# Issuing a gate row's strip products of two weight quarters in a row

## The chip, the cores and the metric

One core of one Trainium2 chip runs the whole program. The metric is the device time of one execution in microseconds (us). The kernel before took 604.39 us, the median of three runs that lay between 603.84 and 604.91 us.

## The reference, cut to what matters

The program is one step of a hybrid trunk layer: a modulated RMS norm, one input projection for two parallel head groups (a gated position-mixing group and a latent attention group), a joint output projection, and a gated residual. Nine tiles of 128 tokens pass through it, eight of latent tokens and one of context tokens. The part that the change touches is the gate:

```python
mod = jax.nn.silu(cond) @ w_ada + b_ada
shift, scale, gate = jnp.split(mod[:, None, :], 3, axis=-1)
...
return x + gate * y
```

`cond` is one vector of 1024 numbers for the latent tokens and another one for the context tokens, `w_ada` is 1024 x 3072. The gate is the last third of the result: two rows of 1024 numbers, one for each condition. Nothing needs it before the output projection at the end of the program.

## The kernel before

The work runs in stages. In the first, the tokens are normed, transposed and modulated, and shift and scale come out of the first two thirds of `w_ada`. In the channel stage twelve chunks of 128 input-projection columns (`w2r` is a raw chunk of 512 KB, `w` its two halves of high and low bits) are multiplied with the modulated tokens, two chunks at a time, as seven sums of products (`p`: p1 to p7) and two plain products for the last three token tiles (`tp`). After that come the wide products (`zacc`), attention, and the output projection.

Every product in the channel stage is a matmul with a 128 x 128 stationary tile and 384 moving columns; a product of fp32 quality is made of three passes. Their results lie in six PSUM banks (pool `psa`). Two further banks (pool `pst`) serve short jobs.

The gate is worked out inside the channel stage, in four quarters of 256 columns, one at a time, by `gate_steps(j)` from line 996 on. One quarter goes as follows.

- `fetch`, lines 1004 to 1008: SyncE's queue loads the quarter of the weights (`adag`, 1 MB) and its bias (`grow`, 2 KB). The pool `vg` has one buffer for `adag`.
- `strips`, lines 1010 to 1014: eight matmuls, one for each 128 rows of the quarter. The stationary tile `csp` is only 32 columns wide (two conditions, the rest zeros), so four of them stand beside each other in the array, and their results go to four strips of 32 partitions of one `pst` bank (`gps`). The trace shows each of these fp32 matmuls as two.
- `high` on ScalarE (line 1018, tile `hig`) and `low` on VectorE (the helper in line 112, tile `log`) split the strips into two parts.
- `total`, line 1026: two matmuls against a selecting matrix add the four strips up to two rows, in the other half of the same bank.
- `out`, lines 1029 and 1030: VectorE adds the bias, and a DMA writes the two rows to the DRAM tensor `gdram`, from where the output projection reads them back at 515 us and later.

The order on each engine is fixed when the program is written out. A planner (class `Plan`, from line 42) takes steps with an engine, an assumed cost, dependences and a priority, and runs through assumed time; whenever an engine is free it writes out the first ready step in order of priority. The real engines follow that written order, and wait on semaphores. The names of the steps are `ga` (load), `gr` (strips), `gh`, `gl` (split), `gt` (total) and `go` (out), with the quarter's number. The two tuples in lines 1033 and 1036 tie the strips and the totals to places among the `p` and `tp` products: each may come only after the product named there.

Of the kernel before, what the change touches and what calls it, by code (L numbers as in the profile page):

```python
# [9 lines left out]
F32 = mybir.dt.float32  # L10
# [8 lines left out]
P = 128  # L19
# [75 lines left out]
def tile_hymba_step(ctx: ExitStack, tc: tile.TileContext, I, O):  # L95
    nc = tc.nc
    V, S, G, T = nc.vector, nc.scalar, nc.gpsimd, nc.tensor

    def opened(name, bufs=1, space=None, side=None):
        kw = dict(name=name, bufs=bufs, reuse_waits="tile")  # L100
        if space is not None:
            kw["space"] = space
        if side is not None:
            kw["side"] = side
        cm = tc.tile_pool(**kw)
        return cm, cm.__enter__()
# [4 lines left out]
    def lo_of(lo, src, hi):  # L111
        V.tensor_tensor(lo, src, f32(hi), op=ALU.subtract)  # L112
# [58 lines left out]
    def catch_up(until):  # L171
        at_ = now[0]
        while waiting and waiting[0][0] <= until:
            due, fn = waiting.pop(0)
            now[0] = due
            fn()
        now[0] = at_
# [9 lines left out]
    def step(cost, fn):  # L187

        catch_up(now[0])
        for f in list(fill):  # L190
            if f[0] in made and made_at[f[0]] <= now[0]:
                fill.remove(f)
                run(f[1:])
        run((cost, fn))
# [12 lines left out]
    def run(step):  # L207
        catch_up(now[0])
        step[1]()
        now[0] += step[0]  # L210
# [16 lines left out]
    c_pc, pc = opened("pc", side="right")  # L227
# [3 lines left out]
    c_pt, pst = opened("pst", bufs=2, space=PSUM)  # L231
# [131 lines left out]
    ada = {}  # L363
# [276 lines left out]
    step = plan.add  # L640

    def bank(pool, tag, name):
        return pool.tile([P, 512], F32, tag=tag, name=name)
# [28 lines left out]
    def load_step(key, fn, deps, prio, cost=1.46):  # L672
        step(key, "D", cost, fn, deps, prio, lag=2.0)
# [81 lines left out]
    pools, opened_as = {}, {}  # L755
# [242 lines left out]
    def gate_steps(j):  # L998


        cell = {}
        prio = 8 + 0.1 * j

        def fetch():
            cell["w"] = pools["vg"].tile([P, 8, 256], F32, tag="ada", name=f"adag{j}")
            nc.sync.dma_start(cell["w"], I["ada_g"][j])
            cell["row"] = pools["vg"].tile([2, 256], F32, tag="row", name=f"grow{j}", bufs=2)
            nc.sync.dma_start(cell["row"], I["b_gate"][j : j + 1, :].rearrange("a (c r) -> (a c) r", c=2))

        def strips():  # L1010
            cell["ps"] = bank(pst, "t", f"gps{j}")
            for kk in range(NK):
                s_, i = kk % 4, kk // 4
                T.matmul(cell["ps"][32 * s_ : 32 * s_ + 32, 0:256], csp[:, kk, :], cell["w"][:, kk, :], start=i == 0, stop=i == 1)

        def high():
            cell["hi"] = pools["vg"].tile([P, 256], F32R, tag="hig", name=f"hig{j}")
            S.copy(cell["hi"], cell["ps"][:, 0:256])

        def low():  # L1020
            cell["lo"] = pools["vg"].tile([P, 256], F32R, tag="log", name=f"log{j}")
            lo_of(cell["lo"], cell["ps"][:, 0:256], cell["hi"])

        def total():
            for m in range(2):
                T.matmul(cell["ps"][0:2, 256:512], selr, cell[("hi", "lo")[m]], start=m == 0, stop=m == 1)

        def out():
            V.tensor_tensor(cell["row"], cell["ps"][0:2, 256:512], cell["row"], op=ALU.add)
            nc.sync.dma_start(gdram[:, 256 * j : 256 * j + 256], cell["row"])  # L1030

        load_step(f"ga{j}", fetch, ["vg", *([f"gr{j - 1}"] if j else [])], prio, cost=3.6)
        step(f"gr{j}", "T", 0.7, strips, [f"ga{j}", ("p3_2", "tp62", "p1_3", "p6_3")[j]], 4.0, takes=("pst",))
        step(f"gh{j}", "S", 0.4, high, [f"gr{j}"], 1.0)
        step(f"gl{j}", "V", 0.4, low, [f"gh{j}"], 1.0)
        step(f"gt{j}", "T", 0.35, total, [f"gl{j}", ("tp62", "p1_3", "p2_3", "p7_3")[j]], 4.0)
        step(f"go{j}", "V", 0.35, out, [f"gt{j}"], 1.0, gives=("pst",))

    def wide_weights():

# [16 lines left out]
    def all_channels():  # L1057
        def gate_room():
            closed(c_vb)
            open_left("vg")  # L1060

        def mix_b():
            close_left("vg")
            opened_as["mb"], mb = opened("mb", side="right")
            pools["mixB"] = mb.tile([P, 4, NT * P], F32, tag="mixB", name="mixB")

        plan.free["N"] = 0.0
        step("vg", "N", 0.0, gate_room, [f"mix{t}" for t in range(NT)], 0)
        step("mb", "N", 0.0, mix_b, [f"go{j}" for j in range(4)], 0)
        plan.resources.update(ka=1, kc=1, kd=1)  # L1070
        for k in range(4):
            input_sums(k, 2.6 + 0.01 * k)
        for n in range(6):
            pair_steps(n)
        for j in range(4):
            gate_steps(j)
        wide_weights()
        for k in range(4):
            input_back(k, 7 + 0.1 * k, ["p5_5"])
# [39 lines left out]
    wuv = pc.tile([P, 4, P], F32, tag="wuv", name="wuv")  # L1119
# [363 lines left out]
    def score_steps(t, h):  # L1483
        g, j = t // 3, t % 3
        sl = slice(j * P, (j + 1) * P)
        a, b = qnh[g][:, h, sl], qnl[g][:, h, sl]
        unrot = qr[g][:, 1, h, sl]
        c_ = s2[:, h % 2, :]
        rot = qr[g][:, 0, h, sl]
        cell = {}  # L1490

        def lat(half):
            if half == 0:
                cell["s"] = pss.tile([P, 2, 512], F32, tag="s1", name=f"s1{t}{h}", bufs=2)
            logits(cell["s"][:, half, :], (a, b, rot), slice(half * 512, half * 512 + 512))
            if half == 1:
                cell["start"], cell["shift"] = softmax(t, h, cell["s"].rearrange("p a c -> p (a c)"), c_)
                later(1.2, cell["start"])

        def con():  # L1500
            logits(c_, (a, b, unrot), slice(CTX0, CTX0 + 256))
            later(0.95 if t else 0.7, cell["shift"])

        return [(1.08, lambda: lat(0)), (1.08, lambda: lat(1)), (0.55, con)]
# [245 lines left out]
    with tc.manual_schedule(engines=engines):  # L1750
# [168 lines left out]
        first = [s_ for i in range(LEAD) for s_ in score_steps(*heads[i])]  # L1919
# [80 lines left out]
    step = plan.add  # L2000
# [111 lines left out]
    for q in range(3, len(queue)):  # L2112
        n, name, _ = queue[q]
        cell = {}
# [16 lines left out]
    turn = [None]  # L2131
# [260 lines left out]
```

## Time and profile before

| what | value |
|---|---|
| median of three runs | 604.39 us |
| the profiled execution, its own time | 604.54 us |
| its span, first to last instruction | 602.8 us |
| TensorE busy | 592.7 us, 98% |
| VectorE, ScalarE, GpSimd busy | 427.1, 333.5, 213.5 us |
| granted TensorE clock | 0.998 |
| strip matmuls of the gate row | 64 records, 162.7 to 186.6 us |

The profile numbers come from one execution. PE is TensorE's matmuls, PEld its loads of stationary tiles, DVE is VectorE, ACT ScalarE, POOL GpSimd, and SPq SyncE's queue of DMA issues. In a timeline row stand the start in us, the time from the start of the first to the end of the last instruction of the row, the engine, the line, the operation, the tile written and the tiles read, the shapes, the count, and in brackets how long the engine had been idle and what ended that. Matmuls overlap, so the step from one row's start to the next row's start tells more than a row's own time.

### The profile page before, as it was taken

The numbers are of one execution on the slowest core, as the hardware profiler recorded it, in microseconds if no ns is written. First come the engines' busy times: TensorE is split into PE (matmuls) and PEld (weight loads), VectorE is DVE, ScalarE is ACT, GpSimd is POOL, SyncE is SP. The second block draws the span as 40 slices with busy tenths as digits, with TensorE's granted clock in tenths as the row PEclk, the third lists the DMA queues.
The fourth block names the chain that finished last, engine by engine and source line by source line (L and its number), as shares of the span: only waits on it lengthen the run. The fifth ranks groups of instructions, "written<-read, shape, count | busy, mean of one in ns | idle before, by whom it ended". The sixth has DMA issues, their size and how long they took to land.

```text
span 602.8 us, 10190 instructions
## 1 busy us (share of the span) xinstructions
PE 592.7 (98%) x3661; PEld 535.6 (89%) x3661; DVE 427.1 (71%) x940; ACT 333.5 (55%) x773; POOL 213.5 (35%) x251
## 2 busy tenths in 40 slices
PE   8999999999999999999999999999999999999995
PEld 8578889999989999999998999999999998888884
DVE  3666888967646368476678677777788876477885
ACT  6565886434323245455567657665656463457543
POOL 2462103200000000343264254545434447259834
PEclk9999999999999999999999999999999999999999
DMA  8992001032052134100002033434232028951444
GB/s 309 375 348 93 1 2 70 1 139 71 18 201 79 55 93 139 41 1 1 1 8 71 1 120 109 149 116 152 76 125 102 1 71 293 368 177 38 143 147 162
DMA packets 31059, 67.33 MB, mean 112 GB/s; under 512 B 3344, under 2 KB 17440, under 8 KB 29984
## 3 DMA queue, kind: packets, MB, share of 16 engines
q1 hardware_dynamic: 27792, 55.93, 26.6%
q0 software_dynamic: 2352, 8.39, 4.1%
q10 hardware_dynamic: 864, 2.36, 1.2%
q8 instruction: 29, 0.48, 0.3%
q14 instruction: 22, 0.18, 0.1%
HBM read 53.45 MB, written 13.21 MB: 111 GB/s over the span
## 4 chain that ended last, share of the span: by engine, by line
PE 91%; DMA 3%; DVE 2%; POOL 2%; ACT 1%; issue 1%; SPq 0%; POOLq 0%; ACTq 0%
PE p L916 14%; PE tp L937 7%; PE pT L1524 5%; PE s L1477 3%; PE s L1478 3%; PE s L1480 3%; PE s L1479 3%; PE s L1481 3%; PE o L1548 3%; PE o L1549 3%; PE o L1550 3%; PE zacc L1349 2%; PE zacc L1348 2%; PE zacc L1350 2%; PE S L1886 2%; PE S L1885 2%
## 5 line engine op out<-in xcount | busy, mean ns | idle before, releaser
L1463 POOL TENSOR_SCALAR e<-e,rs 128x1280 f32<-128x1280 f32 x32 | 47.2, 1474 | 99.0 <-ACT ph L1528 51.7
L112 DVE TENSOR_TENSOR pl<-pT,ph 128x512 fp32r<-128x512 f32 x81 | 55.5, 687 | 31.3 <-ACT ph L1528 31.3
L1528 ACT CAST ph<-pT 128x512 fp32r<-128x512 f32 x80 | 47.2, 590 | 50.6 <-PE pT L1524 50.0
L1458 ACT ACTIVATE e<-s,nb,scl 128x256 f32<-128x256 f32 x64 | 56.9, 890 | 26.0 <-DVE nb L1446 17.3
L1196 POOL TENSOR_TENSOR kr<-z,rope 128x64 f32<-128x64 f32 x8 | 2.6, 326 | 155.3 <-ACT z L1205 155.3
L937 PE MATMUL tp<-area,w 128*128 128x384 f32 x288 | 52.5, 337 | 0.0
L937 PEld LDWEIGHTS tp<-area,w 128*128 128x128 f32 x288 | 50.4, 188 | 0.0
L1548 PE MATMUL o<-ph,vh 128*128 128x256 f32 x160 | 48.4, 302 | 0.0
L1524 PE MATMUL pT<-ident,e 128*128 128x128 f32 x320 | 47.9, 272 | 0.0
L1549 PE MATMUL o<-pl,vh 128*128 128x256 f32 x160 | 45.0, 281 | 0.0
L1550 PE MATMUL o<-ph,vl 128*128 128x256 f32 x160 | 44.9, 281 | 0.0
L1440 DVE TENSOR_REDUCE m<-s 128x1 f32<-128x1024 f32 x32 | 38.9, 1215 | 2.6 <-PE s L1481 2.6
L1524 PEld LDWEIGHTS pT<-ident,e 128*128 128x128 f32 x320 | 37.7, 140 | 2.6
L1477 PE MATMUL s<-kch,area 128*128 128x512 f32 (+2 forms) x100 | 39.2, 392 | 0.0
L1478 PE MATMUL s<-kcl,area 128*128 128x512 f32 (+2 forms) x100 | 35.4, 354 | 0.0
L1480 PE MATMUL s<-krh,area 128*128 128x512 f32 (+2 forms) x100 | 35.3, 353 | 0.0
L1479 PE MATMUL s<-kch,area 128*128 128x512 f32 (+2 forms) x100 | 35.1, 351 | 0.0
L1481 PE MATMUL s<-krl,area 128*128 128x512 f32 (+2 forms) x100 | 35.0, 350 | 0.0
L1548 PEld LDWEIGHTS o<-ph,vh 128*128 128x128 f32 x160 | 30.1, 188 | 1.8 <-ACT os L1558 0.2
L1549 PEld LDWEIGHTS o<-pl,vh 128*128 128x128 f32 x160 | 30.2, 189 | 1.3
L1550 PEld LDWEIGHTS o<-ph,vl 128*128 128x128 f32 x160 | 30.1, 188 | 0.0
L916 PE MATMUL p<-area,w 128*128 128x384 f32 x144 | 27.7, 338 | 0.0
(687 smaller groups left out, 1741.4 us busy)
## 6 DMA issues: line engine op xcount, KB each, us to landing
ada<-in_ada_ss SPq DMA_DIRECT2D x16, 512.0 KB, 6.8
w2r<-in_w_t SPq DMA_DIRECT2D x12, 512.0 KB, 4.9
x<-in_x SPq DMA_DIRECT2D x9, 512.0 KB, 8.3
adag<-in_ada_g SPq DMA_DIRECT2D x4, 1024.0 KB, 4.8
traw<-in_w_o SPq DMA_DIRECT2D x16, 256.0 KB, 3.5
tdram<-thi SPq DMA_DIRECT2D x32, 128.0 KB, 1.8
tdram<-traw SPq DMA_DIRECT2D x32, 128.0 KB, 1.9
wor<-in_w_o SPq DMA_DIRECT2D x8, 512.0 KB, 3.7
```

Source lines behind the costliest of these rows:

```text
L112: V.tensor_tensor(lo, src, f32(hi), op=ALU.subtract)
L916: T.matmul(banks[key], a_, b_, start=k == 0 and m == 0, stop=k == 3 and m == len(passes) - 1)
L937: T.matmul(tps[c, 2][:, :GW], w_[c][:, k, :], x_[k, 2], start=k == 0 and m == 0, stop=k == NK - 1 and m == 2)
L1458: S.activation(e[:, sl], src, AF.Exp, bias=nb, scale=scl[:, t : t + 1], accum_out=su[:, i : i + 1])
L1477: T.matmul(ps, qh_, kch[:, sl], start=True, stop=False)
L1478: T.matmul(ps, qh_, kcl[:, sl], start=False, stop=False)
L1479: T.matmul(ps, ql_, kch[:, sl], start=False, stop=False)
L1480: T.matmul(ps, qr_, krh[:, sl], start=False, stop=False)
L1524: T.transpose(ps[:, w : w + P], es[t, h][:, c * P : (c + 1) * P], ident)
L1548: T.matmul(o, vh[:, kt, :], ph[:, sl], start=c == 0, stop=False)
L1549: T.matmul(o, vh[:, kt, :], pl[:, sl], start=False, stop=False)
L1550: T.matmul(o, vl[:, kt, :], ph[:, sl], start=False, stop=c == n - 1)
```

## The change

Quarters 0 and 1 have their strips issued one right behind the other, after the first half of p1 of the fourth pair; quarters 2 and 3 have theirs right behind each other ahead of p6 of that pair. The pool `vg` gets two buffers for `adag`, so that two quarters can be there at a time. The bias load is a step of its own (`gb`), and the bias rows lie in a tile of another pool, in the place that the later weight `wuv` takes; quarter j's bias is loaded after the output of quarter j - 2. The totals are tied to other products, and the two `pst` banks now hold two quarters at a time. The matmuls are the same in number and size.

```diff
         def fetch():
-            cell["w"] = pools["vg"].tile([P, 8, 256], F32, tag="ada", name=f"adag{j}")
+            cell["w"] = pools["vg"].tile([P, 8, 256], F32, tag="ada", name=f"adag{j}", bufs=2)
             nc.sync.dma_start(cell["w"], I["ada_g"][j])
-            cell["row"] = pools["vg"].tile([2, 256], F32, tag="row", name=f"grow{j}", bufs=2)
-            nc.sync.dma_start(cell["row"], I["b_gate"][j : j + 1, :].rearrange("a (c r) -> (a c) r", c=2))
...
+        def bias():
+            if j == 0:
+                pools["rows"] = pc.tile([P, 512], F32, tag="wuv", name="grows")
+            cell["row"] = pools["rows"][0:2, 256 * (j % 2) : 256 * (j % 2) + 256]
+            nc.sync.dma_start(cell["row"], I["b_gate"][j : j + 1, :].rearrange("a (c r) -> (a c) r", c=2))
...
-        load_step(f"ga{j}", fetch, ["vg", *([f"gr{j - 1}"] if j else [])], prio, cost=3.6)
-        step(f"gr{j}", "T", 0.7, strips, [f"ga{j}", ("p3_2", "tp62", "p1_3", "p6_3")[j]], 4.0, takes=("pst",))
-        step(f"gh{j}", "S", 0.4, high, [f"gr{j}"], 1.0)
+        first = j % 2 == 0
+        load_step(f"ga{j}", fetch, ["vg", *([f"gr{j - 2}"] if j > 1 else [])], prio, cost=3.0)
+        load_step(f"gb{j}", bias, [f"ga{j}", *([f"go{j - 2}"] if j > 1 else [])], prio, cost=0.6)
+        turn = ["p3_2", "p1_3"][j // 2]
+        if first:
+            waits = [f"ga{j}", f"ga{j + 1}", turn, *(["go1"] if j else [])]
+            step(f"gr{j}", "T", 0.85, strips, waits, 4.0, takes=("pst",))
+        else:
+            step(f"gr{j}", "T", 0.95, strips, [f"|gr{j - 1}"], 0, takes=("pst",))
+        step(f"gh{j}", "S", 0.4, high, [f"gr{j}", *([] if first else [f"gt{j - 1}"])], 1.0)
         step(f"gl{j}", "V", 0.4, low, [f"gh{j}"], 1.0)
-        step(f"gt{j}", "T", 0.35, total, [f"gl{j}", ("tp62", "p1_3", "p2_3", "p7_3")[j]], 4.0)
-        step(f"go{j}", "V", 0.35, out, [f"gt{j}"], 1.0, gives=("pst",))
+        step(f"gt{j}", "T", 0.35, total, [f"gl{j}", ("tp62", "tp62", "p7_3", "p7_3")[j]], 4.0)
+        step(f"go{j}", "V", 0.35, out, [f"gt{j}", f"gb{j}"], 1.0, gives=("pst",))
```

What the planner makes of it stands in the order of the instructions, here on two engines. The first piece is TensorE in the kernel before, around the third and the fourth quarter's strips (`gps_1894`, `gps_1966`); `p_3_1884` is p6 of the fourth pair, `p_3_1917` p7, `p_3_1938` p5, `p_3_1953` p4.

```order
L937 MATMUL tp_1844<-area_120,w_1723 128x384
L916 MATMUL p_3_1884<-w1t,s_3_1670 128x384 x6
L1014 MATMUL gps_1894<-adag_1838,csp 32x256 x8
L916 MATMUL p_3_1884<-w1t,s_3_1670 128x384 x6
L916 MATMUL p_3_1917<-w1t,s_3_1782 128x384 x6
L1026 MATMUL gps_1894<-hig_1909,selr 2x256
L1026 MATMUL gps_1894<-log_1915,selr 2x256
L916 MATMUL p_3_1917<-w1t,s_3_1782 128x384 x6
L916 MATMUL p_3_1938<-area_119,s_3_1703 128x384 x12
```

The second piece is TensorE in the changed kernel at the same place; the strips are `gps_1885` and `gps_1897`, p6 is `p_3_1910`, p7 `p_3_1923`, p5 `p_3_1940`.

```order
L937 MATMUL tp_1843<-area_120,w_1726 128x384
L1012 MATMUL gps_1885<-adag_1768,csp 32x256 x8
L1012 MATMUL gps_1897<-adag_1817,csp 32x256 x8
L916 MATMUL p_3_1910<-w1t,s_3_1673 128x384 x12
L916 MATMUL p_3_1923<-w1t,s_3_1773 128x384 x12
L916 MATMUL p_3_1940<-area_119,s_3_1706 128x384 x6
L1030 MATMUL gps_1885<-hig_1906,selr 2x256
L1030 MATMUL gps_1885<-log_1908,selr 2x256
L916 MATMUL p_3_1940<-area_119,s_3_1706 128x384 x6
```

The third quarter's strips stood between the halves of p6 and the fourth's between the halves of p4; now both stand ahead of p6, and p6 and p7 run through without a break. The third total has moved from p7 to the middle of p5. At the first place it is the same: the second quarter's strips have come forward to the first's, by twelve `p` and 24 `tp` matmuls.

The next two pieces are VectorE between the outs of the first two quarters, before and changed. `w2r_1805` and `w2r_1815` are the same raw chunk, the second of the fifth pair's.

```order
L1029 TENSOR_TENSOR grow_1386<-gps_1742,grow_1386 2x256
L112 TENSOR_TENSOR log_1842<-gps_1819,hig_1836 128x256
L775 TENSOR_TENSOR kx_1857<-p_3_1807,ka_1801 128x384
L775 TENSOR_TENSOR sr_1862<-w2r_1805 128x512
L112 TENSOR_TENSOR w_1860<-w2r_1803,w_1859 128x1024
L1029 TENSOR_TENSOR grow_1764<-gps_1819,grow_1764 2x256
```

And changed:

```order
L1033 TENSOR_TENSOR grows<-gps_1745,grows 2x256
L775 TENSOR_TENSOR sr_1841<-w2r_1815 128x512
L112 TENSOR_TENSOR log_1856<-gps_1759,hig_1839 128x256
L775 TENSOR_TENSOR kx_1862<-p_3_1819,ka_1801 128x384
L778 TENSOR_TENSOR sr_1841<-sr_1841,w2r_1799 128x512
L112 TENSOR_TENSOR w_1859<-w2r_1799,w_1858 128x1024
L1033 TENSOR_TENSOR grows<-gps_1759,grows 2x256
```

The second quarter's `log`, on which its total waits, now stands behind a sum (`sr`) that reads the freshly loaded raw chunk.

The last two pieces are SyncE's queue around the two raw chunks of the fifth pair (`w2r_1803` and `w2r_1805`, changed `w2r_1799` and `w2r_1815`), first in the kernel before.

```order
L1006 DMA adag_1762<-in_ada_g 128x2048
L1008 DMA grow_1764<-in_b_gate 2x256
L375 DMA w2r_1803<-in_w_t 128x1024
L375 DMA w2r_1805<-in_w_t 128x1024
L1030 DMA gdram<-grow_1386 2x256
L1006 DMA adag_1838<-in_ada_g 128x2048
```

And changed:

```order
L1006 DMA adag_1768<-in_ada_g 128x2048
L375 DMA w2r_1799<-in_w_t 128x1024
L375 DMA w2r_1815<-in_w_t 128x1024
L1006 DMA adag_1817<-in_ada_g 128x2048
L1034 DMA gdram<-grows 2x256
L1018 DMA grows<-in_b_gate 2x256
```

At the top of these pieces stands the second quarter's load before, and the third's now: the second's has come forward, ahead of the chunks of the fourth pair. The fourth quarter's 1 MB (`adag_1817`) now follows right behind the two raw chunks.

## The prediction

> **What bounds the kernel now.** The page comes first: the share of TensorE in the span of 602.8 us, and the chain of work that ended last.
>
> ```profile
> PE 592.7 (98%) x3661; PEld 535.6 (89%) x3661; DVE 427.1 (71%) x940; ACT 333.5 (55%) x773; POOL 213.5 (35%) x251
> ...
> PE 91%; DMA 3%; DVE 2%; POOL 2%; ACT 1%; issue 1%; SPq 0%; POOLq 0%; ACTq 0%
> ```
>
> TensorE is busy 98% of the time and makes up 91% of the chain. Busy time is only a hint where matmuls overlap, so the windows view is asked for the stretch that the change rearranges.
>
> ```profile
> 163.00:184.00 21.00, 21.00 (x152) 18.50 (x145) 11.34 (x21) 5.82 (x11) 0.00 (x0) 1.00 0.56 202
> ```
>
> TensorE is busy for all 21.00 us of it, at full clock; VectorE (11.34) and ScalarE (5.82) have room. Here a microsecond of TensorE is a microsecond of the program. So the question is what a strip group takes from the stream of products, which the timeline of TensorE tells by the starts of its rows.
>
> ```profile
> 161.61 1.21 PE L916 MATMUL p<-area,w 128*128 128x384 f32 x6
> 162.75 1.07 PE L1014 MATMUL gps<-adag,csp 128*32 128x256 f32 x16
> 163.75 1.31 PE L916 MATMUL p<-area,w 128*128 128x384 f32 x6
> 164.90 4.35 PE L937 MATMUL tp<-area,w 128*128 128x384 f32 x24
> 169.09 1.21 PE L916 MATMUL p<-area,w 128*128 128x384 f32 x6
> ...
> 170.47 1.07 PE L1014 MATMUL gps<-adag,csp 128*32 128x256 f32 x16
> ...
> 174.70 0.28 PE L1026 MATMUL gps<-hig,selr 128*2 128x256 f32 x1
> ...
> 177.03 1.20 PE L916 MATMUL p<-w1t,s 128*128 128x384 f32 x6
> 178.17 1.07 PE L1014 MATMUL gps<-adag,csp 128*32 128x256 f32 x16
> 179.17 2.36 PE L916 MATMUL p<-w1t,s 128*128 128x384 f32 x12
> 181.36 0.28 PE L1026 MATMUL gps<-hig,selr 128*2 128x256 f32 x1
> ...
> 184.74 1.21 PE L916 MATMUL p<-w1t,w 128*128 128x384 f32 x6
> ...
> 188.04 1.21 PE L916 MATMUL p<-area,s 128*128 128x384 f32 x6
> ```
>
> A product costs (169.09 - 164.90) / 24 = 0.1746 us in an unbroken run. First group: from 161.61 to 164.90 are 3.29 us with twelve products in them (2.10), so the strips cost 1.19. Third: 181.36 - 177.03 = 4.33, less eighteen products (3.14): 1.19. Fourth: 188.04 - 184.74 = 3.30, less twelve products: 1.20. The second, at 170.47, stands behind a pair of totals and has the same own time of 1.07; I take 1.19 for it too. Four groups cost 4 x 1.19 = 4.76 us.
>
> How much of that is the strips, and how much is going in and coming out? Narrow windows on the first group show its four rounds of four strips each; the middle two rows hold two rounds each, and only their starts count.
>
> ```profile
> 162.75 0.42 PE L1014 MATMUL gps<-adag,csp 128*32 128x256 f32 x4
> 162.99 0.61 PE L1014 MATMUL gps<-adag,csp 128*32 128x256 f32 x8
> 163.20 0.61 PE L1014 MATMUL gps<-adag,csp 128*32 128x256 f32 x8
> 163.42 0.40 PE L1014 MATMUL gps<-adag,csp 128*32 128x256 f32 x4
> ```
>
> The rounds start at 162.75, 162.99, 163.20 and 163.42: 0.24 for the first, then (163.42 - 162.99) / 2 = 0.215 each. Four rounds at the steady pace are 0.86 us; the other 1.19 - 0.86 = 0.33 is paid around a group: a late start, a slower first round, 163.75 - 163.42 = 0.33 from the last round to the next product in place of 0.215, and a slow first product.
>
> **The change part by part.** *Strips.* A second group right behind the first goes on at the pace of the rounds and costs 0.86 in place of 1.19. Two pairs save 2 x 0.33 = 0.66 us. The trace of before has no two groups in a row, so this is bounded: at the dear end the second group pays all of 1.19 again (saving 0); at the cheap end its first round, too, runs under the first group's end, and it costs the three steps of 163.42 - 162.75 = 0.67 (saving 2 x 0.52 = 1.04). I take 0.86, because the steady rounds change stationary tile and moving rows each time, just as a second group does; only the bank is new.
>
> [...]
>
> *Totals.* Eight matmuls as before, moved from places among products to other such places: 0. TensorE is then 0.86 us later from the end of the first place on, and from the second group's old place 0.33 us earlier.
>
> *Waits that the new order puts on VectorE.* The second total's old start is 174.70, its new one 174.37.
>
> ```profile
> 170.58 0.41 DVE L1029 TENSOR_TENSOR grow<-gps,grow 2x256 f32<-2x256 f32 x1 [0.20 <-PE gps L1026]
> 172.07 0.42 DVE L112 TENSOR_TENSOR log<-gps,hig 128x256 fp32r<-128x256 f32 x1 [1.08 <-ACT hig L1018]
> ...
> 173.29 0.68 DVE L775 TENSOR_TENSOR sr<-w2r 128x512 f32<-128x512 f32 x1
> 173.89 1.22 DVE L112 TENSOR_TENSOR w<-w2r,w 128x1024 fp32r<-128x1024 f32 x1
> ```
>
> The first out moves with its total by 0.86 to 171.44 and ends at 171.85; then `sr` runs, which needs the fifth pair's second raw chunk; then `log`. Queued behind `sr` are `log`, the combination `kx`, `w` and the second out; TensorE's second total waits for `log`. The chunk was the later of the two issued in the second row here; the traffic of all DMA engines around it is the third.
>
> ```profile
> 163.88 0.33 SPq L1006 DMA_DIRECT2D adag<-in_ada_g  x1
> ...
> 164.68 1.25 SPq L375 DMA_DIRECT2D w2r<-in_w_t  x2
> GB/s 655 151 504 202 403 353 252 454 555 252 555 252 340 227 302 302 227 328 403 353 429 403 429 403 378 378 378 403 403 378 328 302 177 101 76 25 0 0 13 0
> ```
>
> That row covers 165.5 to 172 us in 40 slices of 0.1625; traffic stops after slice 36, at 171.35. Allowing 0.5 us for the signal, `sr` starts at 171.9, `log` follows at 171.9 + 0.68 = 172.6 and ends at 173.0: 1.4 us ahead of 174.37. Cost 0; without that cover, one for one.
>
> *Banks.* The third and fourth group need both banks back. The third starts at 178.17 - 1.14 (its six products) - 0.33 = 176.7, the fourth 0.88 later at 177.6. The second out, behind `log` (173.0), `kx` (0.56), the sum's second half (0.67) and `w` (1.22), ends at about 173.0 + 2.5 + 0.41 = 175.9: 1.7 us early. Cost 0.
>
> *Loads.* The second quarter now loads some 40 us earlier, into its own buffer; the third is issued, as the second was, at about 163.9, ahead of the two chunks, and the fourth behind them, at 164.68 + 1.25 = 165.9. Its 1 MB at the 400 GB/s of the row needs 2.6 us behind the chunks: there by 174.5 against 177.6. Cost 0.
>
> *SyncE's queue.* The third bias waits until the first output is in DRAM, the fourth for the second's; behind them are two outputs and the next raw chunks.
>
> ```profile
> DMA to landing us min/median/max: 4.2/4.3/4.3
> 193.76 0.96 SPq L375 DMA_DIRECT2D w2r<-in_w_t  x2
> ```
>
> The outputs take 4.3 us: issued at 171.9, landed 176.2, the second landed 180.5. The fourth out is due near 186.5 and the chunks at 193.4: cover 6 us and more. Cost 0.
>
> *The split at the first load.* ScalarE and VectorE now split the third pair's first chunk (`w`) before they finish the fourth chunk's `tp`.
>
> ```profile
> 128.42 0.49 ACT L845 ACTIVATE tmp<-tp 128x384 f32<-128x384 f32 x1 [2.89 <-PE tp L937]
> 128.81 1.04 ACT L667 CAST w<-w2r 128x1024 fp32r<-128x1024 f32 x1
> 130.48 0.56 DVE L775 TENSOR_TENSOR ka<-p,ka 128x384 f32<-128x384 f32 x1 [0.38 <-PE p L916]
> ```
>
> `tmp` comes at most 1.04 us later and `ka` under 1 us; both free one of six banks that TensorE next asks for some six products of 2.1 us (twelve matmuls) later. Cost 0.
>
> *Sum.* Profiled execution: 604.54 - 0.66 = 603.88. That execution is 0.15 above the median; against the median, 604.39 - 0.66 = 603.7. TensorE runs the same order behind, and the chain is TensorE's, so the gain is passed on.
>
> **The rivals.** *Nothing saved.* The second group pays the full 1.19 because its bank, or the semaphores it waits for, make it begin afresh. For it: the first round of a group is slower than the others (0.24). Against: that round follows products, and the steady rounds change everything but the bank. Time 604.4.
>
> *Slower: the raw chunk lands late.* The fourth quarter's 1 MB is now right behind the chunk that `sr` waits for. If the transfers are interleaved, the chunk lands up to 2.6 us later: `sr` at 174.5, `log` ends at 175.6, the second total starts 1.2 us late. Time 603.7 + 1.2 = 604.9. It decides from a landing after 171.9 + 1.4 = 173.3. Against: the row at 163.88 shows 1 MB issued just ahead of the chunks, and the row of traffic runs on at the same rate; in such a queue the earlier one would be expected first. [...]
>
> *A better result.* The second group hides its first round: 604.39 - 1.04 = 603.35. For it: entry costs more than the 0.24 of a first round; against: the four strips of a round take the whole array, and steady rounds hide nothing.
>
> **How the numbers follow.** Forecast 603.7: 0.73. Nothing saved 604.4: 0.12. Late chunk 604.9: 0.07. Better 603.35: 0.08. About 0.2% (1.2 us, 603.2 and 605.6) is what a measurement can tell from no change here; the three runs of before lie 0.5 us to either side of their median. None of the cases passes that bound by itself. With half a microsecond of such spread the better case and the forecast's low side reach below 603.2: faster 0.15. A late chunk with more waits behind it reaches 605.6: slower 0.06. Same 0.79. The range takes in all four cases, with the better one's 603.35 less 0.35 of spread, 603.0, and the late chunk's 604.9.
>
> **What would show it.** In the changed trace, two places with 32 strip records each; eight rounds at 0.215 with no longer step between the fourth and the fifth; from the first product before to the second after, about 2.05 us more than the products alone. VectorE's `log` of the second quarter ends by 173.1, TensorE shows no idle time ahead of the second total or the fourth group, and the raw chunks are issued 0.66 us earlier than at 193.76. A step of 0.5 us between the fourth and fifth round would speak for "nothing saved", an idle TensorE at 174.4 for the late chunk. A time below 603.0 or above 604.9 would mean a cost or a gain outside the places named.

## The result, and the profile after

The changed kernel took 603.7 us, the median of 22 runs (603.16 to 604.2), against 604.48 us for the kernel before in as many runs (603.84 to 605.37). The ratio is 0.9986, with a 95% interval from 0.998 to 0.9992: about 0.8 us less, and the interval reaches from 0.5 to 1.2 us. The profiled execution took 603.91 us, its span is 602.0.

The first lines to compare are the page's busy times and the window over the rearranged stretch (the columns are the window, its length, then busy time and count for PE, PEld, DVE, ACT and POOL, the clock, the DMA share and GB/s).

```profile
PE 592.4 (98%) x3661; PEld 536.6 (89%) x3661; DVE 428.4 (71%) x940; ACT 333.0 (55%) x773; POOL 212.9 (35%) x251
```

```profile
163.00:184.00 21.00, 21.00 (x165) 18.65 (x158) 10.83 (x20) 5.92 (x11) 0.00 (x0) 1.00 0.40 152
```

TensorE is still busy for all 21.00 us. No new wait has appeared on it, but it has more instructions in the window than before (165 in place of 152). Busy time tells nothing of a gain here: the page's PE figure has moved by 0.3 us of 592. The gain has to be read from starts. This is TensorE's timeline in the changed kernel.

```profile
161.63 1.21 PE L916 MATMUL p<-area,w 128*128 128x384 f32 x6
162.76 1.93 PE L1012 MATMUL gps<-adag,csp 128*32 128x256 f32 x32
...
165.77 4.32 PE L937 MATMUL tp<-area,w 128*128 128x384 f32 x24
...
174.35 0.28 PE L1030 MATMUL gps<-hig,selr 128*2 128x256 f32 x1
...
174.58 2.26 PE L937 MATMUL tp<-area,w 128*128 128x384 f32 x12
176.77 1.93 PE L1012 MATMUL gps<-adag,csp 128*32 128x256 f32 x32
178.63 4.43 PE L916 MATMUL p<-w1t,s 128*128 128x384 f32 x24
182.90 1.21 PE L916 MATMUL p<-area,s 128*128 128x384 f32 x6
...
191.79 4.40 PE L937 MATMUL tp<-area,w 128*128 128x384 f32 x24
```

First place: from 161.63 to 165.77 are 4.14 us with twelve products in them (2.10), so two groups cost 2.05. Second place: 182.90 - 174.58 = 8.32, less 36 products (6.29): 2.03. Together 4.08, where four groups cost 4.76 in the kernel before. The same 24 `tp` as in the last row stood here in the kernel before:

```profile
192.50 4.40 PE L937 MATMUL tp<-area,w 128*128 128x384 f32 x24
```

At 161.6 the two kernels are level (161.61 and 161.63); behind the last total the changed one is 192.50 - 191.79 = 0.71 ahead. Nearly the whole gain lies between these two points; the span is shorter by 0.8. Now the rounds inside the first pair: four narrow windows. Each row holds two rounds or one, so that only its start counts.

```profile
162.76 0.42 PE L1012 MATMUL gps<-adag,csp 128*32 128x256 f32 x4
163.22 0.61 PE L1012 MATMUL gps<-adag,csp 128*32 128x256 f32 x8
163.65 0.61 PE L1012 MATMUL gps<-adag,csp 128*32 128x256 f32 x8
164.08 0.61 PE L1012 MATMUL gps<-adag,csp 128*32 128x256 f32 x8
```

The starts are those of the first, third, fifth and seventh round. From the third to the fifth, where the second group and the second bank begin, are 0.43 us, exactly what the fifth to the seventh take. The second group has no entry of its own.

VectorE between the two outs is the place where the slower rival would have shown.

```profile
171.41 0.41 DVE L1033 TENSOR_TENSOR grows<-gps,grows 2x256 f32<-2x256 f32 x1 [0.20 <-PE gps L1030]
171.90 0.69 DVE L775 TENSOR_TENSOR sr<-w2r 128x512 f32<-128x512 f32 x1
172.51 0.42 DVE L112 TENSOR_TENSOR log<-gps,hig 128x256 fp32r<-128x256 f32 x1
...
175.04 0.41 DVE L1033 TENSOR_TENSOR grows<-gps,grows 2x256 f32<-2x256 f32 x1
```

`sr` has no bracket: the profile counts no wait for its raw chunk. It came in just then, though: the second chunk was issued at about 165.6, and the DMA view gives it 6.3 us from issue to landing, which is 171.9. `log` ends at 172.93 and TensorE's second total starts at 174.35, 1.4 us later; the second out ends at 175.45, and the next pair of groups starts at 176.77. Last, SyncE's queue.

```profile
164.68 1.27 SPq L375 DMA_DIRECT2D w2r<-in_w_t  x2
...
171.85 0.26 SPq L1034 DMA_DIRECT2D gdram<-grows  x1
173.91 0.24 SPq L1018 DMA_DIRECT2D grows<-in_b_gate  x1
...
192.73 0.96 SPq L375 DMA_DIRECT2D w2r<-in_w_t  x2
```

The third bias left 2.06 us after the first output's issue, not 4.3, and the next raw chunks are issued at 192.73, 1.03 earlier than before.

### The profile page after: what moved, and what is told of

Read it like the earlier page. It is cut to its first block, busy times and chain, and to the rows that moved or that the text cites. A ratio compares the mean times of both kernels' runs of the same rounds, so it can differ in the third digit from the quotient of the medians.

```text
span 602.0 us, 10192 instructions
## 1 busy us (share of the span) xinstructions
PE 592.4 (98%) x3661; PEld 536.6 (89%) x3661; DVE 428.4 (71%) x940; ACT 333.0 (55%) x773; POOL 212.9 (35%) x251
## 4 chain that ended last, share of the span: by engine, by line
PE 91%; DMA 3%; DVE 2%; POOL 2%; ACT 1%; issue 1%; SPq 0%; POOLq 0%; ACTq 0%
PE p L916 14%; PE tp L937 7%; PE pT L1535 5%; PE s L1488 3%; PE s L1491 3%; PE s L1489 3%; PE s L1490 3%; PE s L1492 3%; PE o L1559 3%; PE o L1560 3%; PE o L1561 3%; PE zacc L1360 2%; PE zacc L1361 2%; PE zacc L1359 2%; PE S L1896 2%; PE S L1897 2%
```

## The experiments

The theory: a strip group between products pays some 0.33 us for going in and coming out, and groups in a row pay it once. The rivals: something else in the change (a load, a wait, the order of the split) moved the time; or the 0.33 belongs to the strips' type or length. Every ratio below is against the kernel before, run beside it on the same chip.

**The pairs pulled apart.** The changed kernel with its buffers, loads, bias tile and totals' places, but with each second group later, behind 18 products in the first pair and behind 12 in the second:

```diff
-            step(f"gr{j}", "T", 0.95, strips, [f"|gr{j - 1}"], 0, takes=("pst",))
+            step(f"gr{j}", "T", 0.95, strips, [f"ga{j}", f"gr{j - 1}", ("p1_3", "p6_3a")[j // 2]], 4.0, takes=("pst",))
```

> The changed kernel with its double buffer, its loads and its bias rows, but the second strip group of each pair stands one product behind the first, so that there are four groups again. Theory (a group in a row with another saves the 0.33 us of going in and coming out): back to the time before, 604.4 to 604.5 us, ratio 1.000. Rival (the gain comes from the loads, the second buffer or the new order of the other engines): the changed kernel's 603.7, ratio 0.9986.

Measured: 604.34 us beside 604.34, ratio 1.0 (0.9991 to 1.0009). TensorE's timeline around the first two groups:

```profile
163.41 1.07 PE L1012 MATMUL gps<-adag,csp 128*32 128x256 f32 x16
...
167.75 1.07 PE L1012 MATMUL gps<-adag,csp 128*32 128x256 f32 x16
```

Eighteen products lie between these groups, 167.75 - 163.41 = 4.34 less 3.14 is 1.20: the full price is back, and the gain is gone. So the adjacency makes it; the double buffer, the bias step and the moved totals are together worth nothing by themselves, as far as an interval of some 0.5 us to either side can tell.

**Each group cut in halves.** The other direction: eight places with two rounds each.

```diff
...
-            for kk in range(NK):
+            for kk in range(4 * half, 4 * half + 4):
...
+        step(f"grh{j}", "T", 0.45, lambda: strips(0), waits, 4.0, takes=("pst",))
+        step(f"gr{j}", "T", 0.45, lambda: strips(1), [f"grh{j}", ("p1_3", "p2_3a", "p6_3a", "p7_3a")[j]], 4.0)
...
```

> The changed kernel with every strip group cut into two halves of four matmuls, all eight halves apart from each other by products. Theory: six more goings in and out than in the changed kernel, four more than before, at 0.33 us each: 604.5 + 4 x 0.33 = 605.8 us, ratio 1.0022. Rival (gain from loads, buffer or other engines): 603.7, ratio 0.9986.

Measured: 605.34 us beside 604.34, ratio 1.0013 (1.0004 to 1.0022). The direction is the theory's, the size is 1.0 where the theory had four more times 0.33, 1.3. The timeline says where the rest is.

```profile
169.67 0.64 PE L1013 MATMUL gps<-adag,csp 128*32 128x256 f32 x8
170.24 0.28 PE L1031 MATMUL gps<-hig,selr 128*2 128x256 f32 x1
...
178.88 0.64 PE L1013 MATMUL gps<-adag,csp 128*32 128x256 f32 x8
...
180.70 0.64 PE L1013 MATMUL gps<-adag,csp 128*32 128x256 f32 x8
```

A half between products costs 180.70 - 178.88 = 1.82 less six products (1.05), 0.77, which is two rounds (0.43) and 0.34: the price is the same for half a group. But two of the eight halves (the one at 169.67 and another at 184.32) came to stand right ahead of a total. There the slow first product behind the strips falls away (between products, six of them take 1.15 us behind a half, from 163.49 to 164.64, and 1.05 elsewhere): from the half at 169.67 to the next one at 172.67 are 3.00 us, less twelve products (2.10) and the total (0.24) 0.66 in place of 0.77. That is some 0.1 us each, 0.2 of the 0.3 that is missing; the rest is within the interval.

**All four groups in a row.** Two quarters in each bank, at the first place; the weights of quarters 1 and 2 are read again for 3 and 4, since no more than two fit, so the second half of the gate row and 2 MB of loads are left out.

```diff
...
+            waits = [*(f"ga{m}" for m in range(4)), "p3_2"] if j == 0 else ["|gr1"]
+            step(f"gr{j}", "T", 0.9, strips, waits, 4.0 if j == 0 else 0, takes=("pst",))
...
+            step(f"gr{j}", "T", 0.9, strips, [f"|gr{j - 1}"], 0)
...
```

> All four quarters' strips in a row at the first place, two quarters in one bank. There is room for two quarters of weights only, so the third and fourth read the weights of the first two again, and the second half of the gate row is left out that way, with 2 MB of loads. Theory: one group in place of four, three times 0.33 us saved: 604.5 - 1.0 = 603.5 us, ratio 0.9984, 0.33 under the changed kernel; the rounds run on at 0.216 us through all four. Rival (a long row of strips pays something of its own, such as the refilling of the instruction queue): a slower round at each new quarter, and 603.7 us or more.

Measured: 603.33 us beside 604.34, ratio 0.9979 (0.997 to 0.9988).

```profile
161.32 1.21 PE L916 MATMUL p<-area,w 128*128 128x384 f32 x6
162.46 3.66 PE L1016 MATMUL gps<-adag,csp 128*32 128x256 f32 x64
...
167.19 4.32 PE L937 MATMUL tp<-area,w 128*128 128x384 f32 x24
```

167.19 - 161.32 = 5.87, less twelve products: 3.78, and sixteen rounds of 0.215 are 3.44. Four groups in one place pay 0.34 once. With eight, four, two places and one place the time is +1.0, 0, -0.8 and -1.0 against before: it follows the number of places. The times alone do not settle the single steps, since each has an interval of about 0.5 us to either side; the traces do. From the row of p1 that the first strips cut in two to the first row `p<-area,w` behind all strips and totals, with 132 products in every case, TensorE takes 28.77 us before, 29.86 with eight places, 28.05 with two and 27.76 with one: +1.09, -0.72 and -1.01.

**The fourth quarter's load ahead of the raw chunks.** Only SyncE's order changes: the 1 MB that the changed kernel issues behind the two chunks goes first.

```diff
-                load_step(f"w2r{c}", lambda c=c: load_w2(c), [*(f"s{m}{n - 1}" for m in (range(1, 5) if n == 1 else (3, 4))), f"w2{c - 2}"], 1.35)
+                load_step(f"w2r{c}", lambda c=c: (pools["fetch3"]() if c == 8 else None, load_w2(c)), [*(f"s{m}{n - 1}" for m in (range(1, 5) if n == 1 else (3, 4))), f"w2{c - 2}"], 1.35)
...
-        load_step(f"ga{j}", fetch, ["vg", *([f"gr{j - 2}"] if j > 1 else [])], prio, cost=3.0)
+        if j == 3:
+            pools["fetch3"] = fetch
+        load_step(f"ga{j}", fetch if j < 3 else lambda: None, ["vg", *([f"gr{j - 2}"] if j > 1 else [])], prio, cost=3.0)
```

> The changed kernel with the fourth quarter's 1 MB issued ahead of the fifth pair's two raw chunks in place of behind them; the order on the other engines is the same. Theory (the second total has a cover of some 1.4 us for a late chunk, and what exceeds it delays TensorE one for one): the chunk lands 2.6 us later, at 174.0 to 174.5 us, log ends at 175.3 to 175.6, the second total starts 1.0 to 1.2 us late: 604.7 to 604.9 us, ratio 1.0004 to 1.0007. Rival (the split on VectorE is not on TensorE's path): 603.7, ratio 0.9986.

Measured: 604.91 us beside 604.34, ratio 1.0007 (0.9998 to 1.0015), so the whole gain is lost and perhaps more. First VectorE, then TensorE.

```profile
174.18 0.69 DVE L775 TENSOR_TENSOR sr<-w2r 128x512 f32<-128x512 f32 x1 [2.52 <-DMA w2r<-in_w_t]
```

```profile
172.09 2.25 PE L937 MATMUL tp<-area,w 128*128 128x384 f32 x12
175.26 0.28 PE L1030 MATMUL gps<-hig,selr 128*2 128x256 f32 x1 [0.91 <-DVE log L112]
```

VectorE waits 2.52 us for the chunk, `log` stands behind that wait, and TensorE stands idle for 0.91 us: the chain that the slower rival described, with the cover of 1.4 us taken off. The chain is shown; that it did not happen in the changed kernel is due to the order of two loads in one queue. Matmuls overlap, so the starts tell the cost better than the idle time: from the row of twelve `tp` ahead of it, the second total starts 175.26 - 172.09 = 3.17 us later here, and 174.35 - 172.26 = 2.09 in the changed kernel, so 1.08 are lost. The difference of the two times is 1.35 (+0.57 and -0.78 against their own runs of before); the rest is within the two intervals.

**One accumulating tile in place of four strips.** What is the 0.33 paid for? First idea: for strips that stand beside each other in the array. So the kernel before, with the eight matmuls on two stationary columns, one after another into two rows, without split and totals:

```diff
-                T.matmul(cell["ps"][32 * s_ : 32 * s_ + 32, 0:256], csp[:, kk, :], cell["w"][:, kk, :], start=i == 0, stop=i == 1)
+                T.matmul(cell["ps"][0:2, 256:512], csp[:, kk, 0:2], cell["w"][:, kk, :], start=kk == 0, stop=kk == NK - 1)
...
```

> The kernel before with each quarter's eight matmuls on two columns of the stationary tile and one place in the array, adding up in the bank; there are no strips beside each other, and the split and the totals fall away. The order of TensorE around the groups is that of before. A matmul alone takes the 0.215 us of a round, so a group takes 8 x 0.215 = 1.72 in place of 0.86 and the totals' 0.24 is saved. Theory (the 0.33 us belongs to strips that stand beside each other, not to fp32 matmuls between the others): 4 x (1.72 - 1.19 - 0.24) = 1.16 us more, 605.6, ratio 1.0019. Rival (every fp32 group between products pays 0.33): 4 x (1.72 + 0.33 - 1.19 - 0.24) = 2.5 us more, 607.0, ratio 1.0041.

Measured: 613.59 us beside 604.46, ratio 1.0151 (1.0134 to 1.0168). Both expectations were far too low.

```profile
161.04 1.21 PE L916 MATMUL p<-area,w 128*128 128x384 f32 x6
162.18 3.62 PE L1013 MATMUL gps<-adag,csp 128*2 128x256 f32 x16
...
166.87 4.32 PE L937 MATMUL tp<-area,w 128*128 128x384 f32 x24
```

166.87 - 161.04 = 5.83, less twelve products: 3.74. Sixteen records run one behind the other at 0.215, 3.44 us: both expectations had counted one pass of 0.215 for a matmul, and in fp32 each takes two. The rest, 0.29, is paid although nothing stands side by side. So the idea fell: it is not the strips' neighbourhood. What the strips do save is the length, four records in the time of one.

**A stationary tile of full width.** The same kernel with the 128-column identity in place of the two columns (the gate row isn't computed):

```diff
-                T.matmul(cell["ps"][32 * s_ : 32 * s_ + 32, 0:256], csp[:, kk, :], cell["w"][:, kk, :], start=i == 0, stop=i == 1)
+                T.matmul(cell["ps"][:, 256:512], ident, cell["w"][:, kk, :], start=kk == 0, stop=kk == NK - 1)
...
```

> As the kernel with one place in the array, but with a stationary tile of 128 columns, an identity in place of the condition vectors, so the gate row is left out. The eight fp32 matmuls a group are the same in number and moving columns: 16 records of 0.216, 3.45 us, and no totals (0.24). Theory (going in and out belongs to stationary tiles of at most 32 columns): 4 x (3.45 - 1.19 - 0.24) = 8.1 us more than before, 612.5; the first load of the next stationary tile runs ahead under the last record. Rival (it belongs to fp32 groups of 256 moving columns, wide or narrow): 4 x 0.33 more, 613.8, as with two columns.

Measured: 612.44 us beside 604.43, ratio 1.0135 (1.0121 to 1.0149).

```profile
161.18 1.21 PE L916 MATMUL p<-area,w 128*128 128x384 f32 x6
162.23 3.62 PE L1013 MATMUL gps<-adag,ident 128*128 128x256 f32 x16
...
166.75 4.40 PE L937 MATMUL tp<-area,w 128*128 128x384 f32 x24
```

166.75 - 161.18 = 5.57, less twelve products: 3.48, and the sixteen records are 3.44. Nearly nothing is left over. The loads of stationary tiles show the difference: first two rows of the kernel before, then two of this one.

```profile
162.75 0.59 PEld L1014 LDWEIGHTS gps<-adag,csp 128*32 128x32 f32 x16 [0.25 <-issue]
163.75 1.00 PEld L916 LDWEIGHTS p<-area,w 128*128 128x128 f32 x6 [0.41 <-issue]
```

```profile
162.06 3.38 PEld L1013 LDWEIGHTS gps<-adag,ident 128*128 128x128 f32 x16
165.47 1.12 PEld L916 LDWEIGHTS p<-area,w 128*128 128x128 f32 x6
```

With full-width tiles the load of the next tile starts at 162.06, 0.17 ahead of the first matmul that uses it (162.23), while the last product still runs. With the narrow tile it starts only with its own matmul, at 162.75, after 0.25 us in which the load path waits for nothing that the profile shows; and once more on the way out, 0.41. Out of the full-width group the product's load is early by only 0.02 us (165.47 for 165.49), but the load path does not idle ahead of it.

**Strips in bf16.** The kernel before, whose strips read only the upper halves of the fp32 numbers, in one pass; the low bits of the gate are left out.

```diff
-                T.matmul(cell["ps"][32 * s_ : 32 * s_ + 32, 0:256], csp[:, kk, :], cell["w"][:, kk, :], start=i == 0, stop=i == 1)
+                T.matmul(cell["ps"][32 * s_ : 32 * s_ + 32, 0:256], csp[:, kk, :].bitcast(BF16)[:, 1:64:2], cell["w"][:, kk, :].bitcast(BF16)[:, 1:512:2], start=i == 0, stop=i == 1)
```

> The kernel before with the strips in bf16: both operands are read as the upper halves of their fp32 numbers, so the low bits of the gate are left out. Each matmul is then one record of 256 columns in place of two; the places of the strips in the array are the same. A group's two rounds take about 2 x 0.11 us. Theory (going in and out belongs to the strips of 32 columns, whatever the type): 0.22 + 0.33 = 0.55 in place of 1.19 us a group, four times: 2.6 us less, 601.9. Rival (it belongs to narrow fp32 tiles): 0.22 a group, 3.9 us less, 600.6.

Measured: 601.88 us beside 604.43, ratio 0.9956 (0.9944 to 0.9969).

```profile
161.13 1.21 PE L916 MATMUL p<-area,w 128*128 128x384 f32 x6
162.26 0.41 PE L1014 MATMUL gps<-adag,csp 128*32 128x256 bf16 x8
...
163.75 4.32 PE L937 MATMUL tp<-area,w 128*128 128x384 f32 x24
```

163.75 - 161.13 = 2.62, less 2.10: a group costs 0.52 where it cost 1.19. The records are eight in place of sixteen, so two of the four rounds are gone; rounds in bf16 start 0.12 us apart (the last experiment has four in a row), so two take some 0.25, and 0.52 - 0.25 leaves 0.27 around the group. So bf16 pays nearly the same price: it is not bound to fp32.

**The totals in plain fp32.** The totals also have two columns, yet they show no such price in either kernel: they are of the type fp32r. Here they, `hig`, `log` and the selecting matrix, are plain fp32 in the kernel before.

```diff
...
-            cell["hi"] = pools["vg"].tile([P, 256], F32R, tag="hig", name=f"hig{j}")
+            cell["hi"] = pools["vg"].tile([P, 256], F32, tag="hig", name=f"hig{j}")
...
```

> The kernel before with the totals in plain fp32: the selecting matrix and the two parts are fp32 tiles, so each of the two matmuls of a total is two records; values stay right. Theory (a narrow fp32 stationary tile is what costs 0.33 at its ends, here two columns): a total takes 4 x 0.216 + 0.33 = 1.19 in place of 0.24, four times 0.95 less one shared end at the second group: 3.5 us more, 608.0. Rival (only the strips at several places pay it): 4 x (0.86 - 0.24) = 2.5 us more, 607.0.

Measured: 607.5 us beside 604.43, ratio 1.005 (1.0036 to 1.0063). The time lies between the two expectations, and its interval, 2.2 to 3.8 us, holds both. The trace decides.

```profile
173.49 2.28 PE L937 MATMUL tp<-area,w 128*128 128x384 f32 x12
175.70 0.59 PE L1026 MATMUL gps<-hig,selr 128*2 128x256 f32 x2
...
178.85 1.20 PE L916 MATMUL p<-w1t,s 128*128 128x384 f32 x6
```

178.85 - 173.49 = 5.36, less 24 products (4.19): 1.17 for four records, which are 0.86; the other 0.31 is the price again. The fp32r totals of the changed kernel, from 174.35 to 174.58, take 0.115 us each and no more. So two columns alone do not bring it, and the type alone does not either: it was seen with narrow tiles in fp32 and in bf16, not with narrow fp32r totals, and not with 128 columns in fp32. The load path goes with the price here too:

```profile
175.70 0.09 PEld L1026 LDWEIGHTS gps<-hig,selr 128*2 128x2 f32 x2 [0.25 <-issue]
...
176.66 2.04 PEld L937 LDWEIGHTS tp<-area,w 128*128 128x128 f32 x12 [0.44 <-issue]
```

In the kernel before, the load for the same total in fp32r starts at 174.53, 0.17 us ahead of its matmul (174.70), and no idle time stands around it. That the late load is what makes the price, and not a second sign of one cause, is not shown.

**The changed kernel with strips in bf16.** The version that combines the two gains: the replacement shown above, made in the changed kernel; it leaves out the low bits of the gate, so it is no equal of either kernel.

> The changed kernel with the strips' operands read as the upper bf16 halves of the fp32 numbers, one pass in place of two (the gate loses its low bits). Theory: the price of going into and out of the narrow strips, 0.33 us, is paid once per place, whatever the type and the length of the rounds. A lone bf16 group cost 0.54 us, which is 0.22 of rounds and 0.33 around them, so a pair costs 0.54 + 0.22 = 0.76, and two pairs save 2 x 0.33 = 0.66 against four lone bf16 groups: 601.9 - 0.66 = 601.2 us, ratio to the kernel before about 0.9946, and from the last product before a pair to the second after it 0.76 more than the products alone. Rival: the second group hides under the first only because fp32 rounds are long (0.216 us each); two bf16 rounds are too short to cover the change of bank, and the second group pays its full 0.54: 601.9 us, as without the pairing, ratio 0.9956 or above.

Measured: 601.2 us beside 604.54, ratio 0.9941 (0.9928 to 0.9955): faster than both kernels.

```profile
161.39 1.21 PE L916 MATMUL p<-area,w 128*128 128x384 f32 x6
162.53 0.66 PE L1012 MATMUL gps<-adag,csp 128*32 128x256 bf16 x16
...
164.26 4.32 PE L937 MATMUL tp<-area,w 128*128 128x384 f32 x24
```

164.26 - 161.39 = 2.87, less 2.10: a pair costs 0.77, 0.25 more than a lone bf16 group. Narrow windows show the first of the four rounds at 162.53 and the fourth at 162.90, three steps of 0.12, and the row of sixteen records takes 0.66 where the lone group's eight took 0.41, 0.25 for two rounds more. So the second group pays its two rounds and next to nothing else, short as they are; the rival, which had it pay its full price again, fell.

## Why the prediction was right

*The bound.* The step "a microsecond of TensorE is a microsecond of the program" held: 0.71 us gained by 192 us in the program, 0.8 in the span, 0.8 in the medians. The last 0.1 lies outside the stretch compared and within the interval.

*The price of a group.* Forecast 2.05 for a pair, measured 2.05 and 2.03; rounds forecast at 0.215, measured 0.215, without a longer step between the groups. The gain was forecast as 0.66, and the two places give 4.76 - 4.08 = 0.68; the medians give 0.78, whose interval (0.5 to 1.2) holds it. The rivals "nothing saved" and "a better result" would have given 1.19 and 0.67 for the second group; 2.05 - 1.19 = 0.86 is neither.

*What the price is.* The prediction took the 0.33 as a sum of four small delays without a cause, and the runs name none; they give conditions. In fp32 it vanishes when the stationary tile is as wide as the products' (3.48 us for records of 3.44), and with two columns it is there, 0.29 for the one accumulating tile and 0.31 for the totals. The fp32r totals, also two columns wide, show no price (0.115 us each). So the width of the tile does not decide it alone, and what else does is not shown.

*The waits on VectorE.* `log` was forecast to end at 173.0 and ended at 172.93; the cover was 1.4 us by both. The second out was forecast at 175.9 and ended at 175.45. The late chunk was a real danger: with the load ahead of it the price was 1.08 us on TensorE, where the prediction had put 1.2. The prediction shows no row for the 0.5 us that it allowed for the chunk's signal. Two loads of 1 MB in the kernel before can stand beside it: issued at 171.79 and 179.30, they landed 4.8 and 4.7 us later, some 0.6 and 0.35 us after their traffic had stopped in the DMA view (175.95 and 183.65, in slices of 0.15). The landing at 171.9 is the time that came out with it. Whether the chunks overlapped a little with the load behind them is not shown: the trace gives the landing alone.

*Loads, banks and the split.* All costed at nothing, and at nothing they came: TensorE is level with the kernel before at 161.6, past the moved split and the earlier load, and has no idle time in the window behind it.

*Where a reading was wrong, without effect.* SyncE's queue was costed with 4.3 us from an output's issue to its landing. That row was asked by the tile `gdram`, and so takes in the loads that read it; the DMA view of before shows whose landing it is.

```profile
own<-gdram ACTq DMA_DIRECT2D x1, 256.0 KB, 4.3
...
gdram<-grow SPq DMA_DIRECT2D x4, 2.0 KB
```

The 4.3 is that of a load of 256 KB late in the program, and the 4.2 that of another; for the four outputs of 2 KB no landing is given. The two waits for outputs in the changed kernel are shorter:

```profile
SPq L1018 <- DMA gdram<-grows: 2.6, 2, 1.7
```

Two waits, 2.6 us in all. The cost of nothing held because the cover, 6 us and more, was wide; the figure itself had no ground.

The raw chunks are issued 1.03 us earlier than at 193.76, not 0.66 (the 193.4 that the queue was costed with counts one of the two savings only). TensorE accounts for 0.71 of that, and VectorE for the rest: the chunks wait for the split `s`, and in the kernel before the fourth out stood ahead of it at 191.06. In the changed kernel that out runs at 186.96, and `s` starts at 192.02 in place of 193.06.

## What to carry to other kernels

Price a short odd group in a dense stream of matmuls by the starts of the rows on both sides, not by its own time: here 0.33 of 1.19 us lay around the group and in the product behind it. If a TensorE-bound program has several such groups, put them in a row, and count places, not matmuls. Then check what the new order queues behind a load: the same gain was lost (604.91 us in place of 603.7) when one DMA issue moved ahead of two others.

## What the hardware did that was not expected

- A stationary tile of 2 or 32 columns among tiles of 128 cost 0.29 to 0.34 us for going in and out in fp32, for two rounds as for sixteen, and nearly the same in bf16 (0.27 for the first group). With fp32r totals of 2 columns (0.115 us each) and with fp32 tiles of 128 columns (3.48 us for records of 3.44) it did not appear. What decides this is not settled; strips in fp32r were not tried.
- At such a boundary the load of the next stationary tile no longer ran ahead: 0.25 and 0.41 us of idle time on the load path, against a load that began 0.17 us ahead of its matmul with full-width tiles and with the fp32r totals.
- Half a strip group right ahead of an fp32r total cost 0.66 us, and 0.77 between products: the slow first product behind the strips (0.1 us) was missing.
- Two fp32 totals of 2 columns and a strip group of 32 columns, right behind each other, paid the price once: from 169.37 to 173.49 in the run with fp32 totals are 4.12 us, and less twelve products (2.10), four records of the totals and four rounds of strips (0.215 each, 1.72) 0.30 is left.
- A plain fp32 matmul of 256 moving columns took two records of 0.215 us each, whether its stationary tile had 2 columns or 128; four strips of 32 columns went through in the time of one.
